# Splitting a transformer encoder's weights 1024 columns at a time instead of 512

## The chip, the cores and the metric

The kernel runs on one core of a Trainium2 chip, as one program. The metric is the device time of one execution in microseconds, as the median of several runs. The engines are TensorE (PE; its weight loads are PEld), VectorE (DVE), ScalarE (ACT), GpSimd (POOL) and SyncE (SP), which here only issues DMAs.

## The reference

A trunk of two encoder layers over 256 tokens of width 1024, in float32, with 16 heads of 64 in the mixers and feed-forward width 2816:

```python
def rms_norm(x, g):
    y = xf * lax.rsqrt(jnp.mean(xf * xf, axis=-1, keepdims=True) + EPS)
    return (y * g.astype(jnp.float32)).astype(x.dtype)

def swiglu(h, w_gate, w_up, w_down):
    return (jax.nn.silu(h @ w_gate) * (h @ w_up)) @ w_down

# per layer:  x += 0.5*swiglu(rms_norm(x)); x += mixer(rms_norm(x)); x += 0.5*swiglu(rms_norm(x))
# layer 0, even mixer: one projection -> global attention with rotary | windowed attention with a sink -> out projection
# layer 1, odd mixer: neighbourhood attention over the token grid with a relative bias -> out projection
```

A last rms_norm follows. The four feed-forward passes hold most of the weights: gate and up are 1024 x 2816 each, down is 2816 x 1024.

## The kernel before, in words

The 256 tokens are two tiles of 128. x stays in SBUF; all weights come from HBM once, in the order of use.

Each fp32 product is done by three matmuls on operands that are split in two parts: hi is the operand rounded to the type fp32r, lo is what is left. `mm` multiplies a 128x128 piece of an activation (`h`, `l`) with a 128-row piece of a weight (`wh`, `wl`), three times into the same PSUM bank: h·wh, h·wl, l·wh (L311, L312 and L313). These triples are most of PE's work.

**The weights' way.** `plan` lists units of up to 1 MB: four k-tiles of 128 rows by 512 (or 384) columns of gate, up and the projections, or two row tiles by 1024 columns of down. The very first gate's columns come as units of 1, 1, 2, 2 and 2 k-tiles (`FIRST`). `load` starts a unit's DMA on SP into one of three `raw` buffers and cuts it into pieces of 512 (or 384) columns, class `Piece`. `supply` takes the next piece: ACT copies raw to hi (`high_part`, L319), and DVE later subtracts, lo = raw − hi (`low_part`, L322, two inputs from SBUF). `low` issues that second step, at the next tick or where a matmul needs it. The first piece of a unit also starts the load of a further unit. `PIECES` = 15 buffers hold hi and lo, and at most `AHEAD` = 14 pieces are live: split, and not yet used by both token tiles.

**Order of the work.** The order on PE, ACT, DVE and SP is the order in which the Python code issues (`ORDERED`); POOL's is left to a scheduler. After each triple of matmuls `tick` runs: it issues the pending lo, steps the side tasks whose waiting counts are over, and adds `rate` to `due`; where `due` has reached 1 and fewer than `AHEAD` pieces are live, it supplies a piece. `rate` is 0.53 in the feed-forward, 0.48 in the even and 0.51 in the odd mixer. The side tasks are generators that do all that is not a weight matmul: sums of squares and rstd of a row, transposes (PE) with their split to `th` (ACT, L351) and `tl` (DVE, L356), silu (ACT, L500) and the gate product glu (DVE, L505) with its transposes (PE, L394), and the mixers' rotary, softmax and attention.

**Start.** `first_gates` runs the first gate's eight k-tiles: for each pair of k-tiles it transposes x (L465), splits the result to th and tl, supplies the two weight pieces, and runs the triples of a pair while the next pair is prepared.

**Mixers.** Keys of the even mixer are rotated on POOL (`kra`, `krb`, L717; `t`, L700, and `qr`, L715, are steps of the rotary on DVE or POOL) and transposed (L764); queries are stacked into `qTb`. In the odd mixer `okTz` and `okTx` are the hi and lo part of stacked keys, split from a `tp` bank by ACT and DVE; `p` is a block of softmax (ACT, L666), transposed on PE (L688) and copied back by ACT as `pt` (L584); `ot_02h` and `ot_10h` are hi parts of attention outputs. PSUM banks: two of `pj`, three of `s`, one of `o`, two of `tp`.

Of the kernel before, what the change touches and what calls it, by code (L numbers as in the profile page):

```python
# [9 lines left out]
F32R = mybir.dt.float32r  # L10
# [6 lines left out]
P = 128  # L17
T = 256
NT = 2
D = 1024  # L20
# [8 lines left out]
SCALE = HD ** -0.5  # L29
FF_CHUNKS = [512, 512, 512, 512, 384, 384]  # L30

PIECES = 15
AHEAD = 14
RATE = 0.53
EVEN_RATE = 0.48
ODD_RATE = 0.51
# [19 lines left out]
AHEAD_START = 8  # L56
# [9 lines left out]
}  # L66


class Piece:


    def __init__(self, raw, uses, first):
        self.raw, self.uses, self.first, self.parts = raw, uses, first, None


def constants():
# [46 lines left out]
class Trunk:  # L123
# [4 lines left out]
    def __init__(self, ctx, tc, a, out):  # L128
        self.ctx, self.tc, self.nc, self.a, self.out = ctx, tc, tc.nc, a, out
        pool = lambda name, bufs, **kw: ctx.enter_context(tc.tile_pool(name=name, bufs=bufs, **kw))  # L130
        self.one = pool("one", 1)
        self.ph = None
        self.raw = pool("raw", 3)
        self.wp = pool("wp", PIECES)

        self.two = pool("two", 2)
        self.acc = pool("acc", 1, space=PSUM)
        self.n = 0
        self.rate = RATE
        self.tasks, self.last, self.last_v, self.late = [], [], [EPS] * NT, []  # L140
        self.units, self.whole, self.queue, self.live, self.due, self.half = self.plan(), [], [], 0, 0, None
# [45 lines left out]
    def tick(self, supply=True):  # L187
        self.low()
        for task in list(self.tasks):
            task[0] -= 1  # L190
            if task[0] <= 0 and task[1] is not None:
                self.step(task)
        if supply:
            self.due += self.rate
            if self.due >= 1 and self.live < AHEAD:
                self.due = min(self.due - 1, 1)
                self.supply()
# [60 lines left out]
    def load(self):  # L258
        unit = next(self.units, None)
        if unit is None:  # L260
            return
        pieces, nk, w, uses = unit
        if nk * w > 512:
            raw = self.raw.tile([P, nk, w], F32, tag="raw", name=self.name("raw"))
        else:
            raw = self.t([P, nk, w], "raw", 2)
        for sl, src in pieces:
            self.nc.sync.dma_start(raw[sl], src)
        new = [
            Piece(raw[:, k, c : min(c + 512, w)], uses[c // 512], k + c == 0) for k in range(nk) for c in range(0, w, 512)  # L270
        ]
        self.whole += new
        self.queue += new

    def supply(self):

        self.low()
        if not self.whole:
            return
        piece = self.whole.pop(0)  # L280
        if piece.first:
            self.load()
        w = piece.raw.shape[-1]
        hi = self.wp.tile([P, w], F32R, tag="hi", name=self.name("hi"))
        lo = self.wp.tile([P, w], F32R, tag="lo", name=self.name("lo"))
        self.high_part(hi, piece.raw)
        piece.parts = (hi, lo)
        self.half = piece
        self.live += 1

    def low(self):
# [10 lines left out]
        return got  # L302

    def mm(self, ps, lh, piece, first, last, sl=slice(None)):
        while piece.parts is None:
            self.supply()
        if piece is self.half:
            self.low()
        (h, l), (wh, wl) = lh, (t[:, sl] for t in piece.parts)
        mm = self.nc.tensor.matmul  # L310
        mm(ps, h, wh, start=first, stop=False)  # L311
        mm(ps, h, wl, start=False, stop=False)  # L312
        mm(ps, l, wh, start=False, stop=last)  # L313
        piece.uses -= 1
        self.live -= piece.uses == 0
        self.tick()

    def high_part(self, hi, src):
# [116 lines left out]
    def project(self, hT, pieces, tag):  # L435
        ps = self.bank(tag)
        n = len(pieces)
        for k in range(n):
            self.mm(ps[:, : pieces[k].raw.shape[-1]], hT[k], pieces[k], k == 0, k == n - 1)
        return ps  # L440

    def add_to_x(self, tt, sl, ps, scale, last=True):
# [10 lines left out]
    def first_gates(self, W):  # L453

        nc, now = self.nc, self.now
        ps = [self.bank("s") for _ in range(NT)]
        turned = []

        def turn(j):

            banks = [self.bank("pj" if j % 2 else "tp") for _ in range(NT)]
            for tt in range(NT):
                for i in range(2):
                    k = 2 * j + i
                    nc.tensor.transpose(banks[tt][:, i * P : i * P + P], self.x[tt][:, k * P : k * P + P], self.ident)  # L465
            return banks

        def parts(j, banks):
            for tt in range(NT):
                now.hT[tt] += [self.part_h(banks[tt], tt, 0, 2 * j + i, i) for i in range(2)]  # L470
            for i in range(2):
                self.supply()
                for tt in range(NT):
                    self.part_l(banks[tt], tt, 0, 2 * j + i, i, now.hT[tt][2 * j + i])
                self.low()

        parts(0, turn(0))
        for _ in range(FILL):
            self.warm()
        self.due = -AHEAD_START * RATE  # L480
        for tt in range(NT):
            self.spawn(self.row_rstd(tt, now.r), SQ_WAIT[tt])
        for j in range(KD // 2):
            if j + 1 < KD // 2:
                banks = turn(j + 1)
                parts(j + 1, banks)
            for k in (2 * j, 2 * j + 1):
                for tt in range(NT):
                    self.mm(ps[tt], now.hT[tt][k], W[k], k == 0, k == KD - 1)
        return ps  # L490
# [140 lines left out]
    def maxima(self, S, tt, b0, s, sink, bias, scale):  # L631

        nc = self.nc
        m = self.little([P, 2], "m", 6)
        src, by = S, [1.0, 1.0]
        if bias is None:
            nc.vector.tensor_reduce(m, S, axis=AX.X, op=ALU.max, negate=True)
        else:
            grid = lambda t: t.rearrange("p (m k) -> p m k", k=GRID_W)
            src = self.t([P, 2, T], "p", 4)  # L640
            for i in range(2):
                nc.vector.tensor_tensor_reduce(
                    grid(src[:, i, :]), grid(S[:, i, :]), bias(tt, b0 + i, s), 1.0, NEG, ALU.add, ALU.max, m[:, i : i + 1]
                )
            mm = m
            m = self.little([P, 2], "m2", 6)
            nc.vector.tensor_scalar(m, mm, -1.0, None, op0=ALU.mult)
        if scale is not None:
            by = scale(tt, b0, s)
            mm = m  # L650
            m = self.little([P, 2], "m2", 6)
            nc.vector.tensor_tensor(m, mm, by, op=ALU.mult)
            by = [by[:, i : i + 1] for i in range(2)]
        if sink is not None:
            sk = sink[:, s * 4 + b0 : s * 4 + b0 + 2]
            mm = m
            m = self.little([P, 2], "m2", 6)

            nc.vector.scalar_tensor_tensor(m, sk, -1.0, mm, op0=ALU.mult, op1=ALU.min)
        return src, m, by  # L660
# [424 lines left out]
```

## Time and profile before

| | |
|---|---|
| median of 3 runs | 979.89 us (979.39 to 980.45) |
| the profiled execution | 978.92 us, of which its span is 977.1 us |
| PE busy | 965.5 us, 99% of the span, 4908 matmuls and transposes |
| DVE busy | 607.7 us, 62% |
| ACT busy | 546.0 us, 56% |
| POOL busy | 85.7 us, 9% |
| lo by DVE (L322, both widths) | 664 instructions, 423.2 us |
| hi by ACT (L319, both widths) | 664 instructions, 371.9 us |
| DMA | 170 MB read, 54% of the span on the weight queue |

The trace's times count from the span's start. By stage: the first feed-forward to about 200 us (its start until 25 us), the even mixer to 285, the two feed-forwards between the mixers to 655, the odd mixer to 785, the last feed-forward to the end. Busy time overlaps between engines. In a row of the timeline stand start, duration, engine, line, operation, out<-in, sizes and count; in brackets the engine's idle time ahead of it and what ended it. Several equal instructions in a row are shown as one, with their count (x2) and the time from the first's start to the last's end.

### The profile page before, as it was taken

To read this page: it belongs to the slowest core of one execution; us is meant where nothing else is said; L and a number is where in the kernel's file an instruction comes from. 1 tells how busy PE (TensorE), PEld (TensorE's weight loads), DVE (VectorE), ACT (ScalarE), POOL (GpSimd) and SP (SyncE) were. 2 spreads that over 40 slices of the span, in tenths; PEclk is the share of its full clock that TensorE was granted. 3 is DMA by queue.
4 is the path that set the end of the run, shared out by engine and by line. 5 is a ranking of instruction groups with operands and counts; after the bars stand their busy time and mean duration, and the time that the engine had idled before them with its cause. 6 is when DMAs were issued, how large, how long until landed. Compare 5 with 4: busy or idle time off the path is not lost.

```text
span 977.1 us, 13724 instructions
## 1 busy us (share of the span) xinstructions
PE 965.5 (99%) x4908; PEld 818.6 (84%) x4908; DVE 607.7 (62%) x1195; ACT 546.0 (56%) x1152; POOL 85.7 (9%) x152
## 2 busy tenths in 40 slices
PE   9999999999999999999999999999999999999997
PEld 6888998877788889988888899888888888889886
DVE  6565575488866555654655566548879675555643
ACT  7544564477786544544644446447777664545430
POOL 0020000063420000000000000101331000000002
PEclk9999999999999999999999999999999999999999
DMA  8665576554226555766456456646545355547621
GB/s 290 223 205 172 182 251 214 168 135 120 96 91 208 176 157 158 246 215 197 148 176 197 145 173 231 223 153 197 181 128 170 130 172 181 186 131 235 237 87 43
DMA packets 82373, 171.70 MB, mean 176 GB/s; under 512 B 3712, under 2 KB 25216, under 8 KB 82304
## 3 DMA queue, kind: packets, MB, share of 16 engines
q1 hardware_dynamic: 81728, 170.23, 54.0%
q8 instruction: 38, 0.62, 0.3%
q10 hardware_dynamic: 576, 0.59, 0.2%
q14 instruction: 31, 0.25, 0.1%
HBM read 169.76 MB, written 1.05 MB: 175 GB/s over the span
## 4 chain that ended last, share of the span: by engine, by line
PE 95%; DVE 2%; ACT 1%; POOL 1%; issue 1%; DMA 0%; POOLq 0%; ACTq 0%
PE pj L311 14%; PE pj L313 14%; PE pj L312 14%; PE s L313 13%; PE s L312 13%; PE s L311 13%; PE tp L394 2%; PE o L311 2%; PE o L312 2%; PE o L313 2%; PE o L609 2%; PE tp L688 1%; PE tp L366 1%; PE s L624 1%; PE s L625 1%; DVE lo L322 1%
## 5 line engine op out<-in xcount | busy, mean ns | idle before, releaser
L322 DVE TENSOR_TENSOR lo<-raw,hi 128x512 fp32r<-128x512 f32 (+1 forms) x664 | 423.2, 671 | 239.1 <-ACT hi L319 235.0
L319 ACT ACTIVATE hi<-raw 128x512 fp32r<-128x512 f32 (+1 forms) x664 | 371.9, 606 | 169.4 <-PE s L313 102.4
L311 PE MATMUL pj<-hi,th 128*128 128x512 f32 (+1 forms) x512 | 197.8, 386 | 0.0
L313 PE MATMUL pj<-hi,tl 128*128 128x512 f32 (+1 forms) x512 | 192.8, 377 | 0.0
L312 PE MATMUL pj<-lo,th 128*128 128x512 f32 (+1 forms) x512 | 192.5, 376 | 0.0
L311 PE MATMUL s<-hi,th 128*128 128x512 f32 (+1 forms) x400 | 152.1, 380 | 0.0
L313 PE MATMUL s<-hi,tl 128*128 128x512 f32 (+1 forms) x400 | 149.2, 373 | 0.0
L312 PE MATMUL s<-lo,th 128*128 128x512 f32 (+1 forms) x400 | 148.9, 372 | 0.0
L313 PEld LDWEIGHTS pj<-hi,tl 128*128 128x128 f32 x512 | 96.1, 188 | 15.5
L311 PEld LDWEIGHTS pj<-hi,th 128*128 128x128 f32 x512 | 96.4, 188 | 13.0 <-issue 0.3
L312 PEld LDWEIGHTS pj<-lo,th 128*128 128x128 f32 x512 | 96.4, 188 | 12.8
L319 ACT ACTIVATE g_h<-tp 128x512 fp32r<-128x512 f32 (+1 forms) x48 | 27.0, 563 | 126.4 <-PE tp L394 126.4
L313 PEld LDWEIGHTS s<-hi,tl 128*128 128x128 f32 x400 | 75.2, 188 | 11.2
L312 PEld LDWEIGHTS s<-lo,th 128*128 128x128 f32 x400 | 75.3, 188 | 10.5 <-DVE lo L322 0.2
L311 PEld LDWEIGHTS s<-hi,th 128*128 128x128 f32 x400 | 75.3, 188 | 10.1
L313 PE MATMUL s<-hi,g_l 128*128 128x512 f32 (+2 forms) x198 | 73.6, 372 | 0.0
L312 PE MATMUL s<-lo,g_h 128*128 128x512 f32 (+2 forms) x198 | 73.5, 371 | 0.0
L311 PE MATMUL s<-hi,g_h 128*128 128x512 f32 (+2 forms) x198 | 73.5, 371 | 0.0
L505 DVE SCALAR_TENSOR_TENSOR glu<-pj,rstd,silu 128x512 f32<-128x512 f32 (+1 forms) x48 | 33.7, 702 | 45.1 <-PE pj L313 45.1
L500 ACT ACTIVATE silu<-s,rstd 128x512 f32<-128x512 f32 (+1 forms) x48 | 31.4, 654 | 51.1 <-PE s L313 50.6
L331 POOL TENSOR_TENSOR rstd<-var,mhalf 128x1 f32<-128x1 f32 (+2 forms) x16 | 12.9, 808 | 375.8 <-DVE var L329 375.8
L322 DVE TENSOR_TENSOR g_l<-tp,g_h 128x512 fp32r<-128x512 f32 (+1 forms) x48 | 30.8, 642 | 23.1 <-ACT g_h L319 23.1
(245 smaller groups left out, 1133.7 us busy)
## 6 DMA issues: line engine op xcount, KB each, us to landing
raw<-in_ffn_w_down SPq DMA_DIRECT2D x44, 1024.0 KB, 5.0
raw<-in_ffn_w_up SPq DMA_DIRECT2D x32, 1024.0 KB, 5.2
raw<-in_ffn_w_gate SPq DMA_DIRECT2D x30, 1024.0 KB, 5.1
raw<-in_ffn_w_gate SPq DMA_DIRECT2D x16, 768.0 KB, 4.4
raw<-in_ffn_w_up SPq DMA_DIRECT2D x16, 768.0 KB, 4.4
raw<-in_odd_w_qkv SPq DMA_DIRECT2D x12, 1024.0 KB, 5.2
raw<-in_even_w_in SPq DMA_DIRECT2D x4, 1024.0 KB, 5.1
raw<-in_even_w_out SPq DMA_DIRECT2D x8, 512.0 KB, 5.7
```

The lines of the kernel that those rows point to most:

```text
L311: mm(ps, h, wh, start=first, stop=False)
L312: mm(ps, h, wl, start=False, stop=False)
L313: mm(ps, l, wh, start=False, stop=last)
L319: self.nc.scalar.activation(hi, src, AF.Copy)
L322: self.nc.vector.tensor_tensor(lo, src, hi.bitcast(F32), op=ALU.subtract)
L331: nc.gpsimd.tensor_tensor(r[:, :n], v[:, :n], self.mhalf[:, :n], op=ALU.pow)
L366: nc.tensor.transpose(tb[:, j * P : (j + 1) * P], self.x[tt][:, b * P : (b + 1) * P], self.ident)
L394: self.nc.tensor.transpose(tb[:, i * P : (i + 1) * P], src[:, i * P : (i + 1) * P], self.ident)
L500: nc.scalar.activation(s[:, :w], g[:, :w], AF.Silu, scale=self.rstd_of(tt))
L505: nc.vector.scalar_tensor_tensor(m[:, :w], u[:, :w], self.now.r[tt], s[:, :w], op0=ALU.mult, op1=ALU.mult)
L609: self.nc.tensor.matmul(O[64 * s : 64 * s + 64, i * P : i * P + P], v(b0 + i, s, kc), pT[s][:, i, kc, :], start=(kc == 0), stop=(kc == 1),)
L624: nc.tensor.matmul(S[:, i, :], q, kz[s], start=True, stop=False)
```

## The change

One instruction on ACT and one on DVE now split 1024 columns: two neighbouring k-tiles of a unit, or both halves of one row tile of down (768 where the columns are 384 wide). A `Split` holds what is split together, with its hi and lo in one buffer of [128, 2, w]; a `Piece` is its half i. Seven buffers take the place of fifteen half as large, at most seven splits are live, `due` grows at half the rate, and a split stays live until both halves are used by both token tiles. The DMA units stay as they are. The two units of one k-tile at the very start are still split 512 wide, and `first_gates` supplies once for a pair.

```diff
-PIECES = 15
-AHEAD = 14
+SPLITS = 7
+AHEAD = 7
...
-        self.wp = pool("wp", PIECES)
+        self.wp = pool("wp", SPLITS)
...
-            self.due += self.rate
+            self.due += self.rate / 2
...
-        new = [
-            Piece(raw[:, k, c : min(c + 512, w)], uses[c // 512], k + c == 0) for k in range(nk) for c in range(0, w, 512)
-        ]
-        self.whole += new
-        self.queue += new
+        if w == D:
+            views = [raw[:, k, :].rearrange("p (a w) -> p a w", a=2) for k in range(nk)]
+        else:
+            views = [raw[:, k : min(k + 2, nk), :] for k in range(0, nk, 2)]
+        for n, view in enumerate(views):
+            a = view.shape[1]
+            split = Split(view, sum(uses[i % len(uses)] for i in range(a)), n == 0)
+            self.whole.append(split)
+            self.queue += [Piece(split, i) for i in range(a)]
...
-        hi = self.wp.tile([P, w], F32R, tag="hi", name=self.name("hi"))
-        lo = self.wp.tile([P, w], F32R, tag="lo", name=self.name("lo"))
+        hi = self.wp.tile([P, a, w], F32R, tag="hi", name=self.name("hi"))
+        lo = self.wp.tile([P, a, w], F32R, tag="lo", name=self.name("lo"))
...
-        (h, l), (wh, wl) = lh, (t[:, sl] for t in piece.parts)
+        (h, l), (wh, wl) = lh, (t[:, piece.i, sl] for t in split.parts)
...
-        piece.uses -= 1
-        self.live -= piece.uses == 0
+        split.uses -= 1
+        self.live -= split.uses == 0
...
             for i in range(2):
-                self.supply()
+                if W[2 * j + i].split.parts is None:
+                    self.supply()
...
-        self.due = -AHEAD_START * RATE
+        self.due = -AHEAD_START * RATE / 2
```

In numbers of instructions: before, ACT and DVE each split 536 pieces of 512 and 128 of 384 columns; now each makes 267 splits of 1024, 64 of 768 and 2 of 512, 331 instructions fewer. The order of PE and of SP stays the same.

At the start, on DVE, the second pair of k-tiles stands like this before (tl are lo parts of x's transposes, from `pj` and then `tp` banks):

```order
L356 SCALAR_TENSOR_TENSOR tl_159<-pj_152,mats,th_158 128x128
L356 SCALAR_TENSOR_TENSOR tl_165<-pj_153,mats,th_164 128x128
L322 TENSOR_TENSOR lo_173<-raw_104,hi_172 128x512
L356 SCALAR_TENSOR_TENSOR tl_162<-pj_152,mats,th_161 128x128
L356 SCALAR_TENSOR_TENSOR tl_168<-pj_153,mats,th_167 128x128
L322 TENSOR_TENSOR lo_179<-raw_104,hi_178 128x512
```

and now:

```order
L369 SCALAR_TENSOR_TENSOR tl_159<-pj_152,mats,th_158 128x128
L369 SCALAR_TENSOR_TENSOR tl_165<-pj_153,mats,th_164 128x128
L335 TENSOR_TENSOR lo_173<-raw_104,hi_172 128x1024
L369 SCALAR_TENSOR_TENSOR tl_162<-pj_152,mats,th_161 128x128
L369 SCALAR_TENSOR_TENSOR tl_168<-pj_153,mats,th_167 128x128
L369 SCALAR_TENSOR_TENSOR tl_202<-tp_195,mats,th_201 128x128
```

The lo of the pair's second k-tile has moved ahead into the instruction for its first.

In the odd mixer, on ACT, the place where the second tile's keys are split and attention outputs and softmax blocks follow, before:

```order
L319 ACTIVATE okTz_1956_7361<-tp_7518 64x4x128
L319 ACTIVATE okTz_1957_7362<-tp_7518 64x4x128
L319 ACTIVATE ot_02h_7542<-o_7504 128x256
L319 ACTIVATE hi_7549<-raw_7059 128x512
L666 ACTIVATE p_7492,sums_7464<-p_7492,m_1995_7495 128x256 x2
L584 ACTIVATE pt_7572<-tp_7513 128x512
```

and now:

```order
L332 ACTIVATE okTz_1464_6376<-tp_6522 64x4x128
L332 ACTIVATE okTz_1465_6377<-tp_6522 64x4x128
L332 ACTIVATE hi_6539<-raw_6115 128x1024
L332 ACTIVATE ot_02h_6546<-o_6508 128x256
L680 ACTIVATE p_6496,sums_6472<-p_6496,m_1497_6499 128x256 x2
L598 ACTIVATE pt_6572<-tp_6517 128x512
```

The hi instruction is twice as wide and stands ahead of ot_02h. On DVE at the same place, before:

```order
L647 TENSOR_SCALAR m_1995_7495<-m_7491 128x2
L322 TENSOR_TENSOR lo_7498<-raw_7003,hi_7497 128x512
L322 TENSOR_TENSOR lo_7526<-raw_7059,hi_7525 128x512
L322 TENSOR_TENSOR okTx_1958_7363<-tp_7518,okTz_1956_7361 64x4x128
L322 TENSOR_TENSOR okTx_1959_7364<-tp_7518,okTz_1957_7362 64x4x128
L322 TENSOR_TENSOR lo_7550<-raw_7059,hi_7549 128x512
```

and now:

```order
L661 TENSOR_SCALAR m_1497_6499<-m_6495 128x2
L335 TENSOR_TENSOR lo_6502<-raw_6067,hi_6501 128x1024
L335 TENSOR_TENSOR lo_6540<-raw_6115,hi_6539 128x1024
L335 TENSOR_TENSOR okTx_1466_6378<-tp_6522,okTz_1464_6376 64x4x128
L335 TENSOR_TENSOR okTx_1467_6379<-tp_6522,okTz_1465_6377 64x4x128
L335 TENSOR_TENSOR ot_02l_6547<-o_6508,ot_02h_6546 128x256
```

Two lo stand ahead of okTx before and now, each now twice as wide, and the second depends on the hi that now stands behind okTz on ACT. The third lo of before is gone from this place.

More of the change, by code (lines that the diff above doesn't have):

```diff
@@ L66, with __init__ @@
 }
-class Piece:
+class Split:
     def __init__(self, raw, uses, first):
         self.raw, self.uses, self.first, self.parts = raw, uses, first, None
+class Piece:
+    def __init__(self, split, i):
+        self.split, self.i, self.w = split, i, split.raw.shape[-1]
 def constants():
@@ L279, in supply @@
             return
-        piece = self.whole.pop(0)
-        if piece.first:
+        split = self.whole.pop(0)
+        if split.first:
             self.load()
-        w = piece.raw.shape[-1]
-        hi = self.wp.tile([P, w], F32R, tag="hi", name=self.name("hi"))
-        lo = self.wp.tile([P, w], F32R, tag="lo", name=self.name("lo"))
-        self.high_part(hi, piece.raw)
-        piece.parts = (hi, lo)
-        self.half = piece
+        _, a, w = split.raw.shape
+        hi = self.wp.tile([P, a, w], F32R, tag="hi", name=self.name("hi"))
+        lo = self.wp.tile([P, a, w], F32R, tag="lo", name=self.name("lo"))
+        self.high_part(hi, split.raw)
+        split.parts = (hi, lo)
+        self.half = split
         self.live += 1
@@ L304, in mm @@
     def mm(self, ps, lh, piece, first, last, sl=slice(None)):
-        while piece.parts is None:
+        split = piece.split
+        while split.parts is None:
             self.supply()
-        if piece is self.half:
+        if split is self.half:
             self.low()
-        (h, l), (wh, wl) = lh, (t[:, sl] for t in piece.parts)
+        (h, l), (wh, wl) = lh, (t[:, piece.i, sl] for t in split.parts)
         mm = self.nc.tensor.matmul
@@ L438, in project @@
         for k in range(n):
-            self.mm(ps[:, : pieces[k].raw.shape[-1]], hT[k], pieces[k], k == 0, k == n - 1)
+            self.mm(ps[:, : pieces[k].w], hT[k], pieces[k], k == 0, k == n - 1)
         return ps
```

## The prediction

> **What bounds the kernel now.** I read the busy line first, then the 40 slices, the chain that ended last, and the windows of the mixers against those of the feed-forward stages.
>
> ```profile
> span 977.1 us, 13724 instructions
> PE 965.5 (99%) x4908; PEld 818.6 (84%) x4908; DVE 607.7 (62%) x1195; ACT 546.0 (56%) x1152; POOL 85.7 (9%) x152
> PE   9999999999999999999999999999999999999997
> PE 95%; DVE 2%; ACT 1%; POOL 1%; issue 1%; DMA 0%; POOLq 0%; ACTq 0%
> ```
>
> TensorE is busy for 99% of the span, in every slice, and is 95% of the chain. VectorE and ScalarE, the two engines that the change relieves, are busy 62% and 56%; they carry 2% and 1% of the chain, some 20 and 10 us. A shorter queue there can therefore save only where TensorE waits for it.
>
> The second table has, by window: length, busy us of PE, PEld, DVE, ACT and POOL with counts, clock, DMA share, GB/s.
>
> ```profile
> 200.00:285.00 85.00, 81.44 (x517) 64.53 (x516) 67.63 (x162) 63.04 (x173) 38.28 (x77) 1.00 0.42 112
> 285.00:655.00 370.00, 370.00 (x1779) 317.85 (x1778) 214.10 (x373) 192.59 (x371) 6.80 (x8) 1.00 0.58 188
> 655.00:785.00 130.00, 129.91 (x751) 106.93 (x750) 103.81 (x266) 96.22 (x232) 25.83 (x27) 1.00 0.48 152
> ```
>
> In 370 us of feed-forward PE has no idle time at all. It lacks 3.6 us in the even mixer (window 200 to 285) and 0.1 in the odd one (655 to 785), where DVE is busy 80% of the time (67.63 of 85, 103.81 of 130).
>
> ```profile
> 345.22 0.39 PE L312 MATMUL pj<-lo,th 128*128 128x512 f32 x1
> 345.45 0.39 PE L313 MATMUL pj<-hi,tl 128*128 128x512 f32 x1
> ```
>
> Matmuls follow each other every 0.23 us, so a triple takes 0.68 us and PE's own work does not change: the change keeps PE's instructions and their order.
>
> **The change, part by part.**
>
> ```profile
> L322 DVE TENSOR_TENSOR lo<-raw,hi 128x512 fp32r<-128x512 f32 x536 | 358.5, 699 | 194.4 <-ACT hi L319 191.6
> L322 DVE TENSOR_TENSOR lo<-raw,hi 128x384 fp32r<-128x384 f32 x128 | 65.3, 554 | 44.6 <-ACT hi L319 43.4
> L319 ACT ACTIVATE hi<-raw 128x512 fp32r<-128x512 f32 x536 | 314.0, 628 | 147.3 <-PE s L313 101.9 <-PE pj L313 40.2 <-DMA raw<-in_ffn_w_gate 1.5
> L319 ACT ACTIVATE hi<-raw 128x384 fp32r<-128x384 f32 x128 | 58.6, 517 | 22.0 <-PE pj L313 21.1 <-PE s L313 0.5
> ```
>
> *Price of a wide split.* No row has 1024 columns. From 384 to 512 columns hi grows by 628−517 = 111 ns and lo by 699−554 = 145 ns. Four more steps of 128 give 628+444 = 1.07 us for hi and 699+580 = 1.28 for lo; single lo rows last 0.69, so I take 1.23 to 1.28, that is 1.25. Bounds: no less than the growth alone (0.44 and 0.58 over one narrow piece) and no more than two narrow ones (1.26 and 1.40). What a wide split delays on its queue is thus about 0.44 us on ACT and 0.56 on DVE, per place.
>
> The Trainium skill, "VectorE: DVE Perf Modes", section "The TRN2 errata — SBUF-src ops pay a fixed extra latency per instruction", says that each such DVE instruction pays a fixed sum, so that one large tile beats several small. Its (N+151)/0.96 ns gives 691 ns at 512 (the trace agrees, 0.69) and, as an estimate, 1224 at 1024; the 331 instructions that go would save DVE some 50 us by it. A sum by busy time would make the kernel faster; the sum here stands on what PE waits for.
>
> *Feed-forward, layers' six passes: 0.* hi and lo are made by one supply at half the old rate, seven wide ones ahead instead of fourteen narrow ones. That is the same 14 pieces, at 0.68 us or more each some 9.5 us ahead of use. A wide split finishes (1.07+1.25)−(0.63+0.69) = 1.0 us later than a narrow one, which this lead covers. The other work on these queues is the gate product and the transposes that use it:
>
> ```profile
> 349.95 0.75 DVE L505 SCALAR_TENSOR_TENSOR glu<-pj,rstd,silu 128x512 f32<-128x512 f32 x1 [2.31 <-PE pj L313]
> 353.84 0.60 PE L394 MATMUL tp<-mats,glu 128*128 128x128 f32 x4
> ```
>
> glu ends at 350.70, PE needs it at 353.84: 3.1 us of slack against one wide hi and lo ahead (2.3). The units that SP loads stay the same, in the same order; a raw buffer comes free up to one narrow split later, against DMA busy 0.58 of the window. If the slack were gone, each of 48 glu would show it, at 0.5 us each; I see nothing that takes it.
>
> *Start: +1.5.* The first two pieces (units of one k-tile) stay narrow; k2/k3, k4/k5, k6/k7 become one wide split each, and PE has no lead yet.
>
> ```profile
> 7.04 0.69 DVE L322 TENSOR_TENSOR lo<-raw,hi 128x512 fp32r<-128x512 f32 x1 [0.17 <-ACT hi L319]
> 7.97 0.50 PE L312 MATMUL s<-lo,th 128*128 128x512 f32 x1
> 9.52 1.17 ACT L319 ACTIVATE hi<-raw 128x512 fp32r<-128x512 f32 x2
> 11.33 0.39 PE L312 MATMUL s<-lo,th 128*128 128x512 f32 x1
> 13.85 0.60 PE L465 MATMUL pj<-mats,x 128*128 128x128 f32 x4
> 14.64 1.12 ACT L351 ACTIVATE th<-pj,mats 128x128 fp32r<-128x128 f32 x4
> 15.63 1.16 ACT L319 ACTIVATE hi<-raw 128x512 fp32r<-128x512 f32 x2
> 17.29 0.39 PE L312 MATMUL s<-lo,th 128*128 128x512 f32 x1
> ```
>
> lo's end at 7.73 released PE at 7.97, a lag of 0.24. For k2/k3 the wide hi runs from 9.52 to 10.59, lo (0.05 later) to 11.89, and PE's first use of lo comes at 12.13 instead of 11.33: +0.80. k4/k5 arrive inside that delay: +0. For k6/k7 the transposes move from 13.85 to 14.65 and end at 15.25; th then starts 0.6 later, hi at 16.23 instead of 15.63, ends 17.30, lo 18.60, PE 18.84 against 17.29+0.80 = 18.09: +0.75. Bounds: 0.6 (only the first stall, smaller) to 1.8.
>
> *Odd mixer, first place: +1.1.* A wide hi now stands ahead of ot_02h, the two p and pt, and two wide lo ahead of okTx.
>
> ```profile
> 713.55 1.28 DVE L322 TENSOR_TENSOR lo<-raw,hi 128x512 fp32r<-128x512 f32 x2
> 713.80 1.21 ACT L319 ACTIVATE okTz<-tp 64x512 fp32r<-64x512 f32 x2 [0.86 <-PE tp L394]
> 715.03 0.38 ACT L319 ACTIVATE ot_02h<-o 128x256 fp32r<-128x256 f32 x1
> 715.04 1.39 DVE L322 TENSOR_TENSOR okTx<-tp,okTz 64x512 fp32r<-64x512 f32 x2 [0.21 <-ACT okTz L319]
> 715.31 0.62 ACT L319 ACTIVATE hi<-raw 128x512 fp32r<-128x512 f32 x1
> 716.82 0.58 ACT L584 ACTIVATE pt<-tp 128x512 f32<-128x512 f32 x1
> 716.83 0.60 PE L688 MATMUL tp<-mats,p 128*128 128x128 f32 x4
> ```
>
> PE's transposes at 716.83 fill a tp bank that okTx (to 716.43) or pt gives back. Afterwards pt comes 0.45 later, 717.27 to 717.85, and okTx waits for the second wide lo, whose hi ends near 716.10: lo to 717.35, okTx to 718.7. Whichever bank PE takes, it starts no earlier than 717.85+0.06 = 717.91: +1.08. Bounds: 0 (p comes late anyway) to 1.9 (okTx).
>
> *Odd mixer, second place: +0.45.*
>
> ```profile
> 723.79 0.62 ACT L319 ACTIVATE hi<-raw 128x512 fp32r<-128x512 f32 x1
> 724.31 0.59 ACT L584 ACTIVATE pt<-tp 128x512 f32<-128x512 f32 x1
> 724.96 0.66 PE L688 MATMUL tp<-mats,p 128*128 128x128 f32 x4
> ```
>
> pt ends at 724.90 and PE starts 0.06 later: no slack. hi stays ahead of pt and grows by 0.44. The rest of this mixer gets +0.2 (bounds 0 to 1.2): the slack there is about one wide split.
>
> *Even mixer: +0.5.* POOL's order changes here at two places: two casts of k change places with a multiplication by a table and one by rstd; the same instructions are issued, and I take 0 for it (bounds ±0.5, the length of the krb row below). In this table the columns are who waits, for whom, then us, count and us.
>
> ```profile
> PE tp L764 <- POOL kra L717: 0.9, 1, 0.9
> PE tp L688 <- ACT pt L584: 0.8, 1, 0.8
> PE pj L311 <- DVE t L700: 0.8, 1, 0.8
> PE s L624 <- DVE qTb L322: 0.7, 1, 0.7
> PE tp L394 <- DVE qr L715: 0.3, 1, 0.3
> 203.55 0.46 POOL L717 TENSOR_TENSOR krb<-t,t 128x128 f32<-128x128 f32 x1
> 211.36 0.99 POOL L717 TENSOR_TENSOR kra<-t,t 128x128 f32<-128x128 f32 x1
> ```
>
> Here PE waits 3.5 us, on short work that queues behind splits. An instruction that arrives at any time finds a split running for mean length squared over twice the period. With 664 splits in 977 us (1.47 us each) that is 0.69²/2.94 = 0.16 us before and 1.25²/5.88 = 0.27 after: +0.1 for each of five waits. Bounds: −3.6 (all idle time goes) to +2.8 (each stands behind the 0.56 more of a wide lo).
>
> The sum: 0+1.55+1.1+0.45+0.2+0.5 = +3.8 us. The profiled execution took 978.92, of which 977.1 are span; the sum gives 982.7 for it. The median of the runs is 979.89, 0.97 above it: 983.7.
>
> **Rivals.**
>
> *Port contention in the even mixer, slower still.* kra beside wide DVE work took 0.99 against krb's 0.46 apart from it. A lo of 1.25 holds POOL 0.56 longer than one of 0.69; over the four or five rope and bias steps behind which PE waits that is +2.5: 986.2. For it: the 0.9 wait for kra. Against: half as many lo, so half as many collisions. The Trainium skill, "SBUF — State Buffer", section "Who interferes with whom", states the rule: of a DVE instruction with two SBUF inputs and a GpSimd one, the first holds the port for its whole length. The kra row bears it out as far as a doubled time can.
>
> *Hidden anyway, no change.* The places of the odd mixer have cover that I miss, and the start loses only the first 0.8: +0.8 to 1.0, 980.8. For it: 0.1 us of idle PE in that whole window. Against: the zero slack at 724.96.
>
> *Faster.* In the even mixer all idle time goes, 3.6 us by its window, since VectorE has 331 fewer instructions and its queue runs ahead; the start still costs 1.55 and the odd mixer nothing: −2.1, 977.8. It decides only where nearly all of the 3.6 goes, as the start takes back 1.55 and the bound is 2.0. For it: those five waits end on DVE, ACT and POOL work that stands behind splits. Against: they are chains of several short steps (sums, rope, transposes), and what those steps take themselves stays.
>
> **How the numbers follow.** A measurement here can tell about 0.2%, 2.0 us, from no change. Forecast (982 to 985.5, likeliest 983.7) 0.53; contention 0.15; hidden 0.22; faster 0.10. So slower by over 0.2% has 0.68, same 0.22, faster 0.10. The range takes in hidden and contention and leaves out the faster case: 980.0 to 986.6; the forecast's own is 982 to 985.5.
>
> **What would show it.** In the profile after: hi rows of 1.07 and lo of 1.25 us, 267 of each; the matmul on k2's lo at about 12.1 us; PE's transposes after p and pt some 1.1 and 0.45 us later against the triples before; feed-forward windows with PE still full; the waits of the even mixer a few tenths longer. Wrong if a wide lo costs two narrow ones, if DVE or ACT appear as releasers inside feed-forward, or if the even mixer's idle 3.6 us shrinks by more than 1.

## The result and the profile after

The changed kernel takes 986.60 us (median of 6 runs, 986.07 to 986.84) against 980.12 us before (6 runs, 979.39 to 980.63): ratio 1.0066, 95% interval 1.0053 to 1.0079. It is 6.5 us slower. The forecast was 983.7, its range 980.0 to 986.6. The profiled execution of the changed kernel took 986.84 us, span 985.0; that of before 978.92, span 977.1.

The page of the profile after:

```profile
span 985.0 us, 12813 instructions
PE 968.1 (98%) x4908; PEld 819.2 (83%) x4908; DVE 577.7 (59%) x864; ACT 514.1 (52%) x821; POOL 89.7 (9%) x152
PE 89%; DVE 4%; ACT 4%; POOL 2%; issue 1%; DMA 0%; POOLq 0%; ACTq 0%
```

VectorE lost 30 us of busy time and ScalarE 32. Their share of the chain that ended last went the other way, from 2% and 1% to 4% and 4%. The wide splits, grouped by shape:

```profile
L335 DVE TENSOR_TENSOR lo<-raw,hi 128x1024 fp32r<-128x1024 f32 x267 | 326.1, 1232 | 222.4 <-ACT hi L332 218.7
L332 ACT ACTIVATE hi<-raw 128x1024 fp32r<-128x1024 f32 x267 | 278.8, 1058 | 197.8 <-PE s L326 125.4 <-PE pj L326 71.9
```

1.23 us for lo and 1.06 for hi: the prices of the prediction (1.25 and 1.07). The windows of the same stages, moved by the lag that PE has by then:

```profile
202.00:287.00 85.00, 79.13 (x503) 62.43 (x502) 64.87 (x144) 58.32 (x147) 38.89 (x77) 1.00 0.42 113
287.00:660.00 373.00, 373.00 (x1794) 320.28 (x1794) 204.96 (x236) 181.13 (x237) 6.95 (x8) 1.00 0.56 186
660.00:793.00 133.00, 130.47 (x749) 106.64 (x748) 98.45 (x232) 94.70 (x198) 26.20 (x27) 1.00 0.48 151
```

The feed-forward stretch is full as before. PE's idle time grew from 3.6 to 5.9 us in the even mixer and from 0.1 to 2.5 in the odd one. What PE waited for:

```profile
PE tp L778 <- POOL kra L731: 2.4, 1, 2.4
PE tp L702 <- ACT pt L598: 1.6, 2, 1.0
PE pj L324 <- DVE t L714: 1.1, 1, 1.1
PE s L638 <- DVE oqT L335: 0.9, 1, 0.9
```

Before, the wait for kra was 0.9 us, and there was none for oqT. The two waits for pt lie in the odd mixer, where before there was none: the 0.8 us for pt that the prediction lists is one of the even mixer.

PE runs the same 4908 matmuls in the same order in both programs, so that the n-th row of one trace can be set against the n-th of the other. The difference of their start times is PE's lag. This table gives what it grew by in each stage, for the profiled execution of each kernel that is told of below, against that of before:

| kernel | start, to 30 us | even mixer, 205 to 275 | feed-forward, 275 to 686 | odd mixer, 686 to 771 | median of runs, us |
|---|---|---|---|---|---|
| changed | 2.1 | 2.6 | −0.1 | 3.3 | 986.6 |
| hold_odd | 2.4 | 3.6 | 0.0 | 1.1 | 984.2 |
| wide_8 | 1.7 | 2.5 | 0.0 | 3.2 | 986.2 |
| lo_wide | 1.5 | 2.7 | 0.0 | 4.0 | 988.0 |
| hi_wide | 0.1 | 1.5 | 0.0 | 5.1 | 986.4 |
| two_instr | −0.2 | 0.5 | 0.0 | 3.4 | 982.9 |
| ffn_wide_only | 1.7 | 1.2 | 0.3 | 4.8 | 988.1 |
| n_even | 2.0 | 1.5 | 0.3 | 3.0 | 985.8 |
| n_odd | 1.3 | 2.6 | 0.0 | 4.8 | 990.2 |
| two_hold | 0.2 | 0.5 | 0.0 | 1.9 | 982.0 |
| mended | 1.9 | 1.2 | −0.1 | 1.2 | 982.0 |
| before_13 | 0.1 | 0.8 | −0.1 | 0.1 | 981.0 |
| before_lo256 | 0.4 | 0.1 | 0.0 | 0.1 | 979.6 |

Between 30 and 205 us no lag grew by more than 0.02 us. Behind 771 us ffn_wide_only and n_odd lose another 1.9 us, the others at most 0.1. The 0.3 of ffn_wide_only and n_even in the feed-forward's column are lost at 279 us, still in the even mixer. The column of the start holds, beside the kernel's own loss, matmuls that run at about half speed in the first microseconds, for longer in one execution than in another (last section). At the matmul that takes k2's lo (11.33 before) they make 1.3 us of the lag in hold_odd, mended and ffn_wide_only, 1.0 in the changed kernel and 0.9 in n_even, 0.6 in wide_8, 0.4 in before_lo256 and 0.3 or less in the rest. Of the changed kernel's 7.84 us, 0.97 are of this kind; the 6.9 that are left go with the 6.5 of the medians.

**Even mixer, kra.** GpSimd's rows after, and before:

```profile
208.21 1.65 POOL L344 TENSOR_TENSOR rstd<-var,mhalf 128x2 f32<-128x2 f32 x1 [1.97 <-DVE var L342]
209.94 0.40 POOL L773 TENSOR_TENSOR ka<-ka,rstd 128x128 f32<-128x128 f32 x1
210.41 0.64 POOL L437 CAST kTbx<-kTbz 64x128 fp32r<-64x128 f32 x2
211.12 2.36 POOL L714 TENSOR_TENSOR t<-ka,gtab 128x128 f32<-128x128 f32 x5
213.44 2.06 POOL L714 TENSOR_TENSOR t<-kb,tab 128x128 f32<-128x128 f32 x3
215.46 0.45 POOL L731 TENSOR_TENSOR kra<-t,t 128x128 f32<-128x128 f32 x1
```

```profile
205.72 1.12 POOL L331 TENSOR_TENSOR rstd<-var,mhalf 128x2 f32<-128x2 f32 x1 [1.70 <-DVE var L329]
207.39 1.76 POOL L700 TENSOR_TENSOR t<-ka,gtab 128x128 f32<-128x128 f32 x5
209.21 0.63 POOL L424 CAST kTbx<-kTbz 64x128 fp32r<-64x128 f32 x2
209.93 1.47 POOL L700 TENSOR_TENSOR t<-kb,tab 128x128 f32<-128x128 f32 x3
```

And VectorE's after:

```profile
208.07 1.23 DVE L335 TENSOR_TENSOR lo<-raw,hi 128x1024 fp32r<-128x1024 f32 x1
211.94 1.22 DVE L335 TENSOR_TENSOR lo<-raw,hi 128x1024 fp32r<-128x1024 f32 x1 [1.89 <-ACT hi L332]
213.84 1.21 DVE L335 TENSOR_TENSOR lo<-raw,hi 128x1024 fp32r<-128x1024 f32 x1
```

rstd works on two columns, and takes 1.65 us beside a wide lo that runs to 209.30; the five t take 2.36 beside the next and the three t 2.06 beside the third. Less PE's lag of 2.05, rstd starts 0.44 late, it lasts 0.53 longer, the five t last 0.60 longer, and kra ends 1.5 late. The three t and kra together take hardly longer than before (2.5 and 2.4 us). The casts add nothing: now they stand ahead of the five t, before they stood between the five and the three. The other 1.1 us that the even mixer loses come behind kra, in several smaller steps, whose cause is open.

**Odd mixer, the first place**, from the timeline after:

```profile
719.59 1.06 ACT L332 ACTIVATE hi<-raw 128x1024 fp32r<-128x1024 f32 x1
720.69 1.23 DVE L335 TENSOR_TENSOR lo<-raw,hi 128x1024 fp32r<-128x1024 f32 x1 [1.89 <-ACT hi L332]
721.83 1.38 DVE L335 TENSOR_TENSOR okTx<-tp,okTz 64x512 fp32r<-64x512 f32 x2
721.95 0.58 ACT L598 ACTIVATE pt<-tp 128x512 f32<-128x512 f32 x1
722.58 0.66 PE L702 MATMUL tp<-mats,p 128*128 128x128 f32 x4 [1.04 <-ACT pt L598]
```

The wide hi stands ahead of p and pt, PE starts 0.05 us after pt's end, and its lag grows by 1.2 us. At the second place (pt 730.67, PE 731.32) it grows by 0.6. A third one, at the scores on oqT, was not in the prediction:

```profile
737.62 1.06 ACT L332 ACTIVATE hi<-raw 128x1024 fp32r<-128x1024 f32 x1
738.72 1.79 DVE L335 TENSOR_TENSOR lo<-raw,hi 128x1024 fp32r<-128x1024 f32 x1 [1.89 <-ACT hi L332]
740.52 1.41 DVE L335 TENSOR_TENSOR oqT<-tp,oqT 64x512 fp32r<-64x512 f32 x2
741.35 0.36 PE L638 MATMUL s<-okTz,oqT 128*128 128x256 f32 x1 [0.89 <-DVE oqT L335]
```

VectorE idles 1.89 us for a wide hi, while oqT stands behind the lo; the lo then takes 1.79 beside GpSimd's bias rows. (Each of the 240 lo of this width that run while GpSimd is idle takes 1.21 to 1.23.) The lag grows by 1.05.

### The profile page after: what moved, and what is told of

Its sections match the earlier page's. It is cut to its first block, busy times and chain, and to the rows that moved or that the text cites. A ratio compares the mean times of both kernels' runs of the same rounds, so it can differ in the third digit from the quotient of the medians.

```text
span 985.0 us, 12813 instructions
## 1 busy us (share of the span) xinstructions
PE 968.1 (98%) x4908; PEld 819.2 (83%) x4908; DVE 577.7 (59%) x864; ACT 514.1 (52%) x821; POOL 89.7 (9%) x152
## 3 DMA queue, kind: packets, MB, share of 16 engines
HBM read 169.76 MB, written 1.05 MB: 173 GB/s over the span
## 4 chain that ended last, share of the span: by engine, by line
PE 89%; DVE 4%; ACT 4%; POOL 2%; issue 1%; DMA 0%; POOLq 0%; ACTq 0%
PE pj L324 13%; PE pj L326 13%; PE pj L325 13%; PE s L326 12%; PE s L325 12%; PE s L324 12%; PE tp L407 2%; PE o L324 2%; PE o L325 2%; PE o L326 2%; PE o L623 1%; DVE lo L335 1%; PE tp L702 1%; ACT hi L332 1%; PE tp L379 1%
## 5 line engine op out<-in xcount | busy, mean ns | idle before, releaser
L335 DVE TENSOR_TENSOR lo<-raw,hi 128x1024 fp32r<-128x1024 f32 (+2 forms) x333 | 388.0, 1175 | 261.7 <-ACT hi L332 257.2
L332 ACT ACTIVATE hi<-raw 128x1024 fp32r<-128x1024 f32 (+2 forms) x333 | 333.5, 1015 | 246.2 <-PE s L326 132.5
L325 PEld LDWEIGHTS s<-lo,th 128*128 128x128 f32 x400 | 75.6, 189 | 11.3 <-DVE lo L335 0.8
L344 POOL TENSOR_TENSOR rstd<-var,mhalf 128x1 f32<-128x1 f32 (+2 forms) x16 | 16.8, 1050 | 376.4 <-DVE var L342 376.4
```

Of the source, the lines that this page charges most:

```text
L332: self.nc.scalar.activation(hi, src, AF.Copy)
L335: self.nc.vector.tensor_tensor(lo, src, hi.bitcast(F32), op=ALU.subtract)
L344: nc.gpsimd.tensor_tensor(r[:, :n], v[:, :n], self.mhalf[:, :n], op=ALU.pow)
```

## The experiments

**Wide splits in some stages only.** Three kernels went back to 512 columns in the start and both mixers (ffn_wide_only), in the even mixer alone (n_even), or in the odd mixer alone (n_odd). Room in SBUF was short for both sorts of buffers, so two narrow splits shared one of the seven double buffers, and 13 narrow pieces could be live instead of 14. The rule of the supply, in short:

```diff
-            if self.due >= 1 and self.live < AHEAD:
+            n = len(self.whole[0].pieces) if self.whole else 1      # 1 narrow, 2 wide
+            if self.due >= n and self.live + n <= 14 - (n == 1):
```

> 1024-column splits stay in the feed-forward passes; the first gate's columns and both mixers are split 512 columns at a time again (two narrow splits fill one double buffer, at most 13 live). Theory (the 6.5 us lie in the start and the mixers, feed-forward is free): within 1 us of the kernel before, 979.5 to 981, PE lag against the kernel before under 0.5 us over each feed-forward stretch. Rival (wide splits cost something in feed-forward too, by raw buffers that come free later or by later gate products): 982 or more, with a lag that grows between 25 and 200 or 285 and 655 us.

> As the changed kernel, but the even mixer's weights are split 512 columns at a time. Theory (places add up; PE's lag grew by 2.6 us there): 984.0, 983.4 to 984.6. Rival (lag lost in the even mixer is partly made good or shifted later): 985.5 or more.

> As the changed kernel, but the odd mixer's weights are split 512 columns at a time. Theory (places add up; PE's lag grew by 3.2 us there, at the transposes after p and pt and at the first scores of the second head group): 983.4, 982.8 to 984.0. Rival (the losses come from the wide splits of the feed-forward before and after): no change, 986.

Measured: 988.1 (ratio 1.0084, 1.0070 to 1.0098), 985.8 (1.0058, 1.0045 to 1.0071) and 990.2 (1.0104, 1.0090 to 1.0118). None did as the theory said, and two are slower than the changed kernel. They don't undo the change: with the shared buffers the narrow hi came to stand elsewhere than before. In the odd mixer one stood right behind okTz and another between p and pt. On ACT at the first place, with narrow splits in the odd mixer:

```order
L369 ACTIVATE okTz_1462_6404<-tp_6556 64x4x128
L369 ACTIVATE okTz_1463_6405<-tp_6556 64x4x128
L369 ACTIVATE hi_6571<-raw_6098 128x512
L369 ACTIVATE ot_02h_6578<-o_6542 128x256
L717 ACTIVATE p_6532,sums_6502<-p_6532,m_1497_6535 128x256 x2
L369 ACTIVATE hi_6571<-raw_6098 128x512
L635 ACTIVATE pt_6606<-tp_6551 128x512
```

PE's lag grew by 1.0 and 0.7 us at the two places with splits of half the width: where the hi stands counts, not its width alone. At the first place it was okTx that released PE here (0.9 us): it stands on VectorE behind the lo, which waits for the hi behind okTz. At the second it was pt (0.6). In n_even the wait for kra fell to 0.6, and one for qr grew from 0.3 to 1.8. ffn_wide_only and n_odd also lost 1.6 us at the first matmuls of the last feed-forward, where their splits are wide:

```profile
PE s L362 <- DVE tl L406: 1.3, 2, 0.6
```

In n_odd a wide lo that starts at 788.17 stands ahead of the first of these tl; in the changed kernel one stands there too, but it starts at 785.43, and PE does not wait. So wide splits in feed-forward are free where they fall in the changed kernel, and not wherever they fall. What the shared buffers themselves cost in these three stays open.

**Two instructions for one.** Everything is supplied when the changed kernel supplies it, two pieces at a time, but by two instructions of 512 on each engine (two_instr). In short:

```diff
-        self.high_part(hi, split.raw)
+        for i in range(2):
+            self.high_part(hi[:, i, :], split.raw[:, i, :])       # and low_part likewise
```

> Every split is supplied at the same moments as in the changed kernel, two pieces at a time, but by two instructions of 512 columns on ACT and two on DVE in place of one of 1024. Theory (what costs is that two pieces stand together ahead of the mixers' short work, whatever the number of instructions): as slow as the changed kernel, 986 to 988. Rival (what costs is the long instruction: lo cannot start before the whole hi is done, and a long lo keeps GpSimd off): most of the loss goes, 981 to 983.

Measured: 982.9 (1.0037, 1.0023 to 1.0051). The rival is right on the sum: 3.7 of 6.5 us go. By stage (table) it is right for the start and for kra, where PE even gains 0.6 us on the kernel before; the 1.1 us that the even mixer loses behind kra stay. The theory is right for the odd mixer in the sum, 3.4 us, and at its first two places (1.3 and 0.7). At oqT only 0.25 is lost instead of 1.05, but 0.7 at earlier transposes of p, where the changed kernel loses nothing. So there are two mechanisms at least. Then each engine alone, with only hi wide (hi_wide) and with only lo wide (lo_wide):

> Supplied as in the changed kernel; hi by one instruction of 1024 columns on ACT, lo by two of 512 on DVE. With both narrow in this way the time was 982.9, with both wide 986.6. If the long lo is what costs (GpSimd kept off, short work behind it): near 983, 982.5 to 983.7. If the long hi costs (lo can start only when all of hi is done, 0.5 us later): near 986, 985.3 to 986.7.

> Supplied as in the changed kernel; hi by two instructions of 512 columns on ACT, lo by one of 1024 on DVE. The long lo is taken to cost at the start and at kra in the even mixer (GpSimd kept off its inputs for 1.23 us at a time), since both losses were gone with the narrow lo. Theory: PE's lag grows by about 1 us at the start's last pair and the first up weights, and by 1.3 to 1.7 at kra, as in the changed kernel; 985 to 986.5. Rival (only both long together cost there, since lo must wait for the long hi): lag under 0.7 at each, 983 to 984.

Measured: 986.4 (1.0063, 1.0051 to 1.0076) and 988.0 (1.0085, 1.0070 to 1.0098). The times alone mislead. hi_wide was to tell by its time, and that pointed at the long hi; but its lag at the start and at kra is near 0, and what it loses lies behind kra (1.6) and above all in the odd mixer, 5.1 us against 3.3. lo_wide loses at the start (0.8 at the last pair and 0.5 at the first up weights) and 1.6 at kra, near what the theory said, and again more than the changed kernel in the odd mixer (4.0), so that its time lies above both forecasts. GpSimd's rows with narrow lo (hi_wide):

```profile
206.34 1.12 POOL L381 TENSOR_TENSOR rstd<-var,mhalf 128x2 f32<-128x2 f32 x1 [2.24 <-DVE var L379]
208.72 1.31 POOL L751 TENSOR_TENSOR t<-ka,gtab 128x128 f32<-128x128 f32 x5
209.98 1.92 POOL L751 TENSOR_TENSOR t<-kb,tab 128x128 f32<-128x128 f32 x3
```

rstd is back to 1.12, with the same order on both engines and two lo of 1.29 us together in place of one of 1.23. The five t take 1.31 instead of 2.36: they are through when the next lo starts at 209.99, and it is the three t that run beside that one (1.92). And with wide lo (lo_wide), kra waits as in the changed kernel:

```profile
PE tp L815 <- POOL kra L768: 2.4, 1, 2.4
```

In the changed kernel, in hi_wide and before, rstd ends 0.56 to 0.58 us after the end of the lo that it started beside, be that one of 1.23 us or the first of two of 0.69; with no lo beside it, it takes 0.71 in all (216.29 in the changed kernel). That shows a lo holding GpSimd off until it ends, the longer the wider it is. A kernel whose lo leaves GpSimd's reads alone was not tried. Why one narrow engine beside a wide one makes the odd mixer worse than either kind alone is open.

**The place in the odd mixer.** In hold_odd there is no supply for four ticks from okTz, so that the wide hi stands behind ot_02h, p and pt, and the lo behind okTx:

```diff
+            self.hold -= self.hold > 0
-            if self.due >= 1 and self.live < AHEAD:
+            if self.due >= 1 and self.live < AHEAD and self.hold == 0:
...
             self.high_part(Z[s][HALF[s]], tb[HALF[s]])
+        if self.rate == ODD_RATE:
+            self.hold = 4
```

> The changed kernel, with one addition: in the odd mixer no split is supplied for four ticks from the one that issues okTz, so that the wide hi stands behind ot_02h, p and pt (and the wide lo behind okTx) at both places where PE fell behind. Theory (there the 1.26 and 0.61 us are lost to a wide split that stands ahead of short work): PE's lag at the transposes after p and pt does not grow, 1.9 us are won, 984.7 (984.0 to 985.4). Rival (fewer splits ahead is what costs in the odd mixer, wherever they stand): the same loss or more, later in the mixer, 986.5 or above.

Measured: 984.2 (1.0042, 1.0028 to 1.0056), 2.4 us less than the changed kernel. ACT's order and PE's transposes with the hold:

```profile
719.71 1.21 ACT L333 ACTIVATE okTz<-tp 64x512 fp32r<-64x512 f32 x2 [1.48 <-PE tp L408]
721.23 0.50 ACT L683 ACTIVATE p<-p,m 128x256 f32<-128x256 f32 x1
722.21 0.58 ACT L601 ACTIVATE pt<-tp 128x512 f32<-128x512 f32 x1
722.69 2.00 ACT L333 ACTIVATE hi<-raw 128x1024 fp32r<-128x1024 f32 x2
722.74 0.60 PE L705 MATMUL tp<-mats,p 128*128 128x128 f32 x4
```

PE's lag does not grow at either place (5.91 us ahead of the first, 5.75 behind the second). The width is the same as in the changed kernel; only the place differs.

**The lead.** Does a double buffer, held until both halves are used, leave too few pieces ahead? One kernel is that of before with one piece fewer (before_13), the other the changed kernel with one buffer more (wide_8):

```diff
-AHEAD = 14
+AHEAD = 13
```

> The kernel before with AHEAD = 13 in place of 14: 512-column splits as they were, but one piece fewer may be live. Theory of the lead (the changed kernel holds a double buffer until both halves are used, about one piece less ahead, and in the mixers that alone moves splits behind okTz): the lag grows in the odd mixer by 2 us or more, 982 to 986. Rival (width alone costs): within 0.7 us of the kernel before, 979.5 to 980.9.

```diff
-SPLITS = 7
-AHEAD = 7
+SPLITS = 8
+AHEAD = 8
```

> The changed kernel with eight double buffers and eight splits ahead instead of seven; to make room nat has one buffer and the rows of the bias table two. Theory of the lead: the odd mixer's 3.2 us shrink to 1.5 or less, 984 to 985. Rival (width and place within the tick cost, not the lead): 986 to 987.

Measured: 981.0 (1.0008, 0.9999 to 1.0017) and 986.2 (1.0061, 1.0048 to 1.0074). One piece fewer costs 0.1 us in the odd mixer and 0.8 in the even, 0.55 of it at kra; one split more wins nothing clear in either (3.2 against 3.3, and 2.5 against 2.6). So the lead is not the cause in the odd mixer. In the even mixer it may have a share, which these two runs do not settle.

**Taken together.**

> The changed kernel with its three found losses taken away one by one and nothing else: lo by two instructions of 512 for the first gate's columns and in the even mixer (hi stays 1024 wide), and in the odd mixer no supply for four ticks from okTz. Feed-forward and the odd mixer keep 1024 columns on both engines. Theory (the losses are local and add up, wide splits in feed-forward are free): of 986.6, 0.6 go at the start, 1.6 at kra and 2.2 in the odd mixer: 982.2, 981.6 to 982.8, with no change of PE's lag from 30 to 200 and 290 to 685 us. Rival (wide splits cost in feed-forward or through the lead as well): 983.5 or more.

> Two pieces supplied at a time, by two instructions of 512 on ACT and two on DVE, and in the odd mixer no supply for four ticks from okTz. Theory (the losses add up: 982.9 with narrow instructions, 2.0 to 2.4 us less by the hold): 980.8, 980.2 to 981.4, not clear of the kernel before. Rival (the places overlap, a later one takes over): 982.3 or more.

> The kernel before, with lo in two instructions of 256 columns each in the even mixer alone (54 pieces there). If GpSimd's waits behind lo (p 128x256 took 0.48 us alone, 0.72 beside a lo of 512, 1.01 beside one of 1024) are what PE's wait for kra is made of, the wait of 0.9 us becomes shorter by 0.3 to 0.6: 979.6, 979.0 to 980.1. Rival (some 0.1 us more of DVE for each piece costs more in the queue than GpSimd wins): 980.3 to 981.5.

mended: 982.0 (1.0025, 1.0015 to 1.0035), as forecast. Of the 1.9 us at its start, 1.3 are the slow matmuls of its execution and 0.4 the first up weights, whose lo are still wide. Its feed-forward, with wide splits on both engines:

```profile
30.00:204.00 174.00, 174.00 (x843) 149.79 (x842) 95.88 (x117) 82.81 (x114) 9.47 (x28) 1.00 0.59 192
275.00:686.00 411.00, 411.00 (x2007) 351.31 (x2003) 230.63 (x285) 209.22 (x295) 14.52 (x20) 1.00 0.55 183
```

PE has no idle time in 585 us. two_hold: 982.0 (1.0023, 1.0014 to 1.0033), 1.2 above the forecast: the hold wins 1.5 us in the odd mixer, not 2.0 to 2.4, since the scores on oqT then lose 0.9 instead of 0.3. before_lo256 (in the kernel before, lo in two instructions of 256 in the even mixer): 979.6 against 980.0, ratio 0.9998 (0.9989 to 1.0007); it can't be told from the kernel before. Its wait for kra fell from 0.9 to 0.6 us, and its wait for qTb rose from 0.7 to 0.9. None of these is a version that beats both kernels: in feed-forward, where PE is never idle, there is nothing to win.

## Why the prediction was right or wrong

- *The number: at the edge.* 986.60 is the last value of the range and outside the forecast's own 982 to 985.5; of the 6.5 us the sum had 3.8.
- *Direction and reason: right.* 62 us less busy time on engines that PE doesn't wait for won nothing; a wide split ahead of short work costs. The prices of hi and lo were right within 0.02 us. The estimate that the fewer instructions save VectorE some 50 us was high: the lo rows lost 35 (423.2 to 388.0), since two narrow lo in a row take 1.29 us and not twice 0.69.
- *Feed-forward 0: right* (−0.1 of 411 us, and 373.00 of 373 busy), but by place: in n_odd and ffn_wide_only wide splits cost 1.6 us there.
- *Odd mixer, first place +1.1 and second +0.45: right*, 1.2 and 0.6 measured, and both gone with the hold. PE waited for pt; okTx was not what decided.
- *Rest of the odd mixer +0.2: wrong, about +1.5 measured* (7.84 less 6.36), above its bound of 1.2. The step took the slack there as about one split. 1.05 us of the 1.5 are lost at the scores on oqT, to a lo that waits for its hi and is lengthened by GpSimd's bias rows.
- *Start +1.55: near in size, wrong in part.* k2/k3 was to lose 0.80 to the lo; it lost nothing to it, because k1's hi came 1.0 us sooner (two rows below), and the 0.96 that the profile shows at that matmul are the slow matmuls of this execution (last section). k1's late weights belong to the one execution of before that was profiled: in that of before_13, whose start is the same program, k1's hi waits for nothing and ends at 7.55. k6/k7 lost 0.7 (0.75 forecast), and 0.4 more went at the first up weights, for which the prediction had nothing. So the start's own loss is 1.1, and it is luck that the up weights made up for half of the step that did not come. With narrow lo there and in the feed-forward (hi_wide, two_instr) the start costs 0.1 or nothing. ACT before, where k1's hi waits for its weights, and after:

```profile
7.99 0.63 ACT L319 ACTIVATE hi<-raw 128x512 fp32r<-128x512 f32 x1 [0.98 <-DMA raw<-in_ffn_w_gate]
```

```profile
6.24 1.35 ACT L332 ACTIVATE hi<-raw 128x512 fp32r<-128x512 f32 x2
```

- *Even mixer +0.5: wrong, +2.6 measured.* This is the term that was most mis-sized. Mean waits behind a split, five times 0.1 us, treat VectorE as a queue and leave out GpSimd. The chain to kra crosses it: there a wide lo stops GpSimd's small steps one after the other, 1.5 us in one place (0.44 of it because rstd starts later). The other 1.1 are spread behind it and stay with narrow instructions; their cause is open. The change of GpSimd's order, taken as 0, did cost nothing at kra.
- *The rival of port contention named this at +2.5 over the forecast*, 986.2, with 0.15; measured 986.6. Its mechanism shows in GpSimd's rows, but it explains 1.5 us at kra and at most 0.6 at oqT, where GpSimd lengthens a lo; the rest of the 2.9 us over the forecast came from elsewhere in the two mixers, so that the near number is in part luck. Its rule from the Trainium skill ("SBUF — State Buffer", section "SBUF: two separate sides"), that the other engine is blocked for the whole instruction, agrees with the trace: rstd of 128x2 ended 0.56 us after the lo that it started beside (209.86 and 209.30).
- *Faster, and hidden: wrong.* The even mixer's waits grew, and the two places of the odd mixer had no cover.

## What to carry to other kernels

In this kernel, where one engine is full, fewer and longer instructions on the others won nothing and lengthened what stands in front of short work in their in-order queues: look at each place where the full engine waits, and ask what the longest instruction ahead of the releaser will be. Put bulk work behind the short step of a chain, not ahead of it; in the odd mixer that was worth 2.4 us with no change of width. A long lo on VectorE, with its two inputs in SBUF, also lengthened small GpSimd work beside it, so a chain through GpSimd needs a price of its own.

## What was not expected of the hardware

**The matmul clock at the start.** In the changed kernel's execution the matmuls start 0.43 us apart until 10.4 us:

```profile
8.69 0.63 PE L324 MATMUL s<-hi,th 128*128 128x512 f32 x1
9.12 0.63 PE L325 MATMUL s<-lo,th 128*128 128x512 f32 x1
9.54 0.63 PE L326 MATMUL s<-hi,tl 128*128 128x512 f32 x1
```

In the execution of before they were 0.23 apart from 8.31 on. The profile's clock reads 1.00 in this stretch in both, so the slow clock is read off the spacing alone. In all fourteen profiled executions it ends between 8.1 and 11.3 us, in those of the kernel before and its two variants too (8.3 to 9.2). Narrow splits at the start do not remove it: ffn_wide_only loses 1.3 us there, two_instr nothing. The Trainium skill ("TensorE: Matmul & The Clock Gate", section "Part 1: The HAM clock gate") says that the window which decides this runs free of the kernel, so that the point varies from run to run; that agrees with these executions.

**The same after a stall.** In hold_odd's execution the 2.4 us wait for kra was followed by 3 us at half clock (windows, the clock in the third column from the end):

```profile
216.00:219.40 3.40, 3.12 (x9) 2.43 (x10) 1.07 (x4) 1.08 (x4) 2.86 (x8) 0.51 1.07 230
219.40:223.00 3.60, 3.60 (x19) 3.00 (x18) 3.30 (x7) 1.28 (x2) 1.76 (x6) 0.99 0.08 15
```

PE's lag grew by 1.35 us in these matmuls, 0.5 came back at the next wait, and the mixer ended 1.0 us behind that of the changed kernel (3.6 against 2.6 in the table). That execution took 985.95 us, the other four 983.8 to 984.4. The profiled executions of the changed kernel, of lo_wide and of n_odd had the same wait and kept a clock of 1.00. So a stall of this length cost another 1.0 us once in four executions.
